# Silu by Tanh, scaled probabilities on ScalarE, an earlier residual gate and other small moves in a transformer block with a Fourier branch

## The chip, the cores and the metric

The kernel runs on one core of a Trainium2 chip. The metric is the device time of one execution in microseconds. Times of different kernels are compared by the median of several executions; one further execution is profiled.

## The reference

One layer of a block with two parallel token mixers, for 512 tokens of width 2048 and 256 context tokens, in float32:

```python
h  = modulate(rmsnorm(x, norm_g), shift, scale)         # shift, scale, gate = silu(c) @ w_ada + b_ada
hc = modulate(rmsnorm(ctx, norm_g), shift_c, scale_c)
p  = h @ w_in                  # q | k | v | z_a | u_b | z_b | g_a | g_b
attn = softmax(q k^T) v        # 12 query heads, 4 key heads, 768 keys, q and k normalized and rotated
y_a = (attn * silu(z_a)) @ w_pa
y_b = (real(fft2(u_b)) * silu(z_b)) @ w_pb
y   = (sigmoid(g_a) * y_a + sigmoid(g_b) * y_b) @ w_o
out = rmsnorm(x + gate * y, final_g)
```

## The kernel before, in words

**Precision.** Every matrix is split into a rounded part and a rest: `split_from` (L119 to L121) writes `hi` by ScalarE (L120) and `lo` by VectorE (L121), and `mm3` (L219) makes three matmuls of each product (L221 to L223). The profile names the two halves of a weight `whi` and `wlo`.

**Weights.** All weights are pieces of 128 x 1024 in one list, `todo`, in the order of their use. `start_load` issues a piece on SP's queue (L151) into a free raw tile (`wr`); `get` splits up to `len(hl_pools)` pieces ahead of the one that is asked for. A piece marked `aside` is taken out of turn by `get_aside`. Names are written in the order of the program; the framework that builds the program orders each engine's instructions, gives tiles their addresses and sets the waits. An engine then runs its instructions in that order.

**Stages.** They follow each other in the trace roughly so: modulation and the first products (to 185 us), the Fourier branch and keys and values (to 330), attention (to about 755), the products of the two sigmoid gates (to about 1065), the merge (to 1140 in its first chunks, to 1215 in all), the output product with the final norm (to the end).

**Attention.** The loop at L929 has 48 steps of 128 queries of one head (`scores`, then `turn` for the step before, then `values` for each pair). `scores` reads the maximum on VectorE (L895), makes Exp on ScalarE (L897), takes the reciprocal of the sum and scales the probabilities `p` on VectorE (L898, L899); `turn` transposes them (L906). Between these pieces `fill` advances a generator: first the 21 products of the remaining q heads and of z_a (`mtile`; `silu_into` turns z into Silu by Exp, an addition, a reciprocal and a product, L477 to L480), then the product of the Fourier branch with its weights, which writes sixteen tiles of 128 x 512 (L841, copied by ScalarE from the accumulator) and stores each by POOL's queue to `yb_d` (L842). What is left of the generator when attention ends is run by `fill(64)` (L977), with tiles of another pool, `evp`, that has four tiles of [128, 2, 512].

**The residual gate.** `gate` is a product of silu(c) with 2048 columns of w_ada. It is made on VectorE, row by row: `silu_of_row` (L672) loads half of c as a broadcast row, `crow`, and makes Silu of it by Sigmoid; `gate_piece` (L682) multiplies a 128 x 1024 weight piece by that row and sums it (L684). The first 16 pieces, for the first half of c, run in attention, one in three steps, each loaded two steps before its use. The second 16 run in the merge, where `crow` is loaded a second time; then the sums are added and stored to `gs` by POOL's queue (L1045 to L1047).

**After attention.** Eight loads on POOL's queue (L976) bring back the forms that attention stored in `f_d`. Then come four groups of seven products each (`Group`, a scheme of Strassen's kind that saves one product in eight; P1, Q5, P2, Q6, P7, Q3, Q4), whose accumulators are pairs of banks, tags "x" and "y" with two buffers each. The output product ends with a fifth such group; its last product Q4 is made token tile by token tile (`finish`, L793), and after each half `last` (L1136) forms the sums, the norm and the stores. `rms` takes a square root on ScalarE (L1117).

Of the kernel before, what the change touches and what calls it, by code (L numbers as in the profile page):

```python
# [10 lines left out]
F32 = mybir.dt.float32  # L11
# [7 lines left out]
P = 128  # L19
D = 2048  # L20
T = 512
# [61 lines left out]
def block_kernel(ctx, tc, xT, ctxT, x, c_row, w_ss, w_gate, vecs, qkg, rope, dft_c, dft_s,  # L83
# [218 lines left out]
    S = {}  # L302
    nq = KK
    for n, j in enumerate(CHUNKS):
        for pc in BRANCH_A:
            if n == 0:
                stream(("src", pc), flat(at_d[pc]), 1024, 2, dst=tiles)
            stream(("pab", j, pc), w_pab[j, pc], 1024, 2)
            if 4 <= 6 * n + pc < 20:
                stream(("gate", nq), w_gate[nq], 1024, 1, "raw")  # L310
                todo[-1].aside = True
                nq += 1
    for c in range(2):
# [160 lines left out]

    def silu_into(dst, z, tmp_pool):
        e = tmp_pool.tile([P, T], F32, tag="sil", bufs=1, name=uid("e"))
        nc.scalar.activation(e, z, ACT.Exp, scale=-1.0)  # L477
        nc.vector.tensor_scalar(e, e, 1.0, None, op0=ALU.add)
        nc.vector.reciprocal(e, e)
        nc.vector.tensor_tensor(dst, z, e, op=ALU.mult)  # L480

# [189 lines left out]

    def silu_of_row(half, row, e):  # L672

        nc.gpsimd.dma_start(row, c_row[:, 1024 * half : 1024 * half + 1024].broadcast_to([P, 1024]))
        n = e[0].shape[-1]
        for i, t in enumerate(e):
            r = row[:, n * i : n * i + n]
            nc.scalar.activation(t, r, ACT.Sigmoid)
            nc.vector.tensor_tensor(r, r, t, op=ALU.mult)
        return row  # L680

    def gate_piece(q, row, w):  # L682

        nc.vector.scalar_tensor_tensor(w, w, 1.0, row, op0=ALU.mult, op1=ALU.mult, accum_out=gparts[:, q : q + 1])  # L684

    crow = silu_of_row(0, atp.tile([P, 1024], F32, name="crow"),
                       [atp.tile([P, T], F32, tag="hs", bufs=2, name=uid("cs")) for _ in range(2)])
    later = []
# [46 lines left out]
    def job():  # L735
        if jobs:
            jobs.pop(0)()

    class Group:

# [11 lines left out]
        def run(self, name):  # L752
            form, which = next((f, c) for n, f, _, c in PRODUCTS if n == name)
            start = which not in self.acc
            if start:
                self.acc[which] = pair(self.tags[which])
            a = self.acc[which]
# [56 lines left out]
    def filler():  # L814
# [15 lines left out]
        for j in CHUNKS:  # L830
            w = [get(("pab", j, pc)) for pc in BRANCH_B]
            for t in range(4):
                acc = bank()
                a, s = t // 2, slice((t % 2) * P, (t % 2) * P + P)
                for k in range(4):
                    hi, lo = bsl[k]
                    mm3(acc, hi[:, a, s], lo[:, a, s], w[k // 2][0][:, k % 2, :], w[k // 2][1][:, k % 2, :], k == 0, k == 3)
                    if k < 3:
                        yield
                y = new_yb()  # L840
                nc.scalar.copy(y, acc)  # L841
# [44 lines left out]
    def scores(i):  # L886
# [11 lines left out]
        nc.vector.reciprocal(mx[:, 2:3], mx[:, 1:2])  # L898
        nc.vector.tensor_scalar(p, p, mx[:, 2:3], None, op0=ALU.mult)  # L899
        probs[i] = p  # L900
# [13 lines left out]
    def values(half):  # L914
        h = half // 2
        g = h // GQ
        pth, ptl = pts.pop(half)
        av = bank()
        for k in range(KT):
            s = slice(k * P, (k + 1) * P)  # L920
            mm3(av[:, :256], kvh[:, g, 1, s], kvl[:, g, 1, s], pth[:, k, :], ptl[:, k, :], k == 0, k == KT - 1)
        if half % 2 == 0:
            ats[h] = atp.tile([P, T], F32, tag="at", bufs=2, name=uid("at"))
        c = slice(256 * (half % 2), 256 * (half % 2) + 256)
        nc.vector.tensor_tensor(ats[h][:, c], av[:, :256], zs[h][:, c], op=ALU.mult)
        if half % 2 == 1:
            nc.gpsimd.dma_start(at_d[h // 2, :, h % 2, :], ats[h])

    for i in range(NSTEP + 2):  # L929
# [96 lines left out]

    crow = silu_of_row(1, slot(fm, (1024,)), [slot(fm, (1024,))])
    nq = KK
    for n, j in enumerate(CHUNKS):
# [7 lines left out]
        for pc in BRANCH_A:  # L1037
            if n == 0:
                S[pc] = get(("src", pc))
            wh, wl = get(("pab", j, pc))  # L1040
            if 5 <= 6 * n + pc < 21:
                gate_piece(nq, crow, get_aside(("gate", nq)))
                nq += 1
                if nq == 2 * KK:
                    nc.vector.tensor_tensor(gcol, gparts[:, :KK], gparts[:, KK:], op=ALU.add)  # L1045
                    nc.vector.tensor_tensor(gcol, gcol, bada[:, 2 * KK :], op=ALU.add)
                    nc.gpsimd.dma_start(gs.rearrange("k p -> p k"), gcol)  # L1047
            sh, sl = S[pc]
# [25 lines left out]
    ssq = const.tile([P, 4, 5], F32, name="ssq")  # L1074
    nc.vector.memset(ssq, 0.0)
    new_o = lambda: slot(fm, (2, 512))
# [59 lines left out]
    def last(Y, a, t):  # L1136
# [19 lines left out]
        store(tok, 0)  # L1156


    jobs.insert(0, lambda: form("A22", 0))
# [118 lines left out]
```

## Time and profile before

| | us |
|---|---|
| median of 3 runs (1420.21 to 1423.43) | 1420.81 |
| profiled execution, device time | 1417.62 |
| its span in the profile | 1415.9 |
| TensorE busy | 1367.1 |
| VectorE busy | 963.3 |
| ScalarE busy | 574.0 |
| POOL busy | 101.4 |

The profiled execution is one more run; the 1.7 us between its device time and its span lie outside what the profile covers. Engines are PE (TensorE's matmuls), PEld (its weight loads), DVE (VectorE), ACT (ScalarE), POOL and SP; L120 is line 120 of the kernel. In a group's row stand the line, the engine, the operation, output and inputs, shapes and count, then busy us and mean ns, then the idle time of the engine just before them and what ended it. In a timeline row stand start and duration in us, engine, line, operation, count, and in brackets the idle time before it with its releaser. A DMA row has the queue, the count, the KB of each and the median us from issue to landing.

### The profile page before, as it was taken

What the parts mean: (1) busy time and instruction counts of PE and PEld (TensorE: products, weight loads), DVE (VectorE), ACT (ScalarE), POOL (GpSimd) and SP (SyncE); (2) the same over time, 40 slices, a digit from 0 to 9 for tenths busy, and PEclk for the clock granted to TensorE, in tenths of its full rate; (3) what the DMA queues carried; (4) which work ended last, traced back from release to release, by engine and by line L of the source; (5) the groups of instructions that cost most, each with busy time, mean ns of one, the idle gap of its engine ahead of it and who ended that gap; (6) DMA issues with size and microseconds to landing.
All of it is one profiled execution on the core that took longest, in us unless ns stands there. A gap on an engine that the chain in (4) does not pass through costs nothing.

```text
span 1415.9 us, 17625 instructions
## 1 busy us (share of the span) xinstructions
PE 1367.1 (97%) x6842; PEld 1114.6 (79%) x6842; DVE 963.3 (68%) x1253; ACT 574.0 (41%) x785; POOL 101.4 (7%) x151
## 2 busy tenths in 40 slices
PE   6999999999999999999997999999998999999996
PEld 3667789887888888888886788888886788888874
DVE  4766596867998777777853775666857664437667
ACT  5322253534443444343443644453535122333544
POOL 0000000010011000000012101000010010000100
PEclk9999999999999999999999999999999999999998
DMA  9887453545343322232338798878899984344873
GB/s 362 322 325 273 175 182 112 175 133 169 119 142 126 105 97 83 83 97 88 121 124 351 213 296 237 265 216 255 279 277 329 334 250 139 104 134 149 180 224 131
DMA packets 73795, 275.28 MB, mean 194 GB/s; under 512 B 8560, under 2 KB 9200, under 8 KB 69232
## 3 DMA queue, kind: packets, MB, share of 16 engines
q1 hardware_dynamic: 56160, 212.54, 43.4%
q0 software_dynamic: 13808, 49.30, 13.9%
q10 hardware_dynamic: 3744, 12.32, 2.4%
q8 instruction: 53, 0.87, 0.3%
q14 instruction: 30, 0.25, 0.1%
HBM read 248.95 MB, written 25.17 MB: 194 GB/s over the span
## 4 chain that ended last, share of the span: by engine, by line
PE 70%; DMA 10%; issue 9%; DVE 8%; ACT 1%; POOL 1%; DVEq 0%; SPq 0%; POOLq 0%; ACTq 0%
PE pb L221 9%; PE pb L222 9%; PE pb L223 9%; PE x L222 6%; PE x L223 6%; PE x L221 6%; PE y L222 5%; PE y L221 5%; PE y L223 5%; DMA wr<-in_w_gate 3%; PE pd L221 2%; PE pd L223 2%; PE pd L222 2%; PE pd L392 2%; DVE wlo L121 2%
## 5 line engine op out<-in xcount | busy, mean ns | idle before, releaser
L120 ACT ACTIVATE whi<-wr 128x1024 fp32r<-128x1024 f32 x188 | 195.7, 1045 | 362.8 <-PE pb L222 91.3
L121 DVE TENSOR_TENSOR wlo<-wr,whi 128x1024 fp32r<-128x1024 f32 x188 | 225.6, 1204 | 145.0 <-ACT whi L120 144.3
L221 PE MATMUL pb<-hh,whi 128*128 128x512 f32 x512 | 207.4, 407 | 2.3 <-ACT hh L382 2.3
L222 PE MATMUL pb<-hl,whi 128*128 128x512 f32 x512 | 201.8, 394 | 0.0
L223 PE MATMUL pb<-hh,wlo 128*128 128x512 f32 x512 | 201.2, 393 | 0.0
L222 PE MATMUL y<-wlo,s 128*128 128x512 f32 x348 | 137.2, 394 | 4.4 <-DVE wlo L121 4.4
L221 PE MATMUL y<-whi,s 128*128 128x512 f32 x348 | 136.6, 392 | 2.0 <-DVE s L1144 2.0
L223 PE MATMUL y<-whi,s 128*128 128x512 f32 x348 | 136.4, 392 | 0.0
L221 PEld LDWEIGHTS pb<-hh,whi 128*128 128x128 f32 x512 | 96.6, 189 | 23.2 <-ACT hh L382 3.4
L223 PEld LDWEIGHTS pb<-hh,wlo 128*128 128x128 f32 x512 | 96.4, 188 | 22.4 <-issue 1.8
L222 PEld LDWEIGHTS pb<-hl,whi 128*128 128x128 f32 x512 | 96.9, 189 | 18.1 <-issue 1.6
L222 PE MATMUL x<-wlo,s 128*128 128x512 f32 x248 | 97.5, 393 | 2.3 <-DVE wlo L121 2.3
L221 PE MATMUL x<-whi,s 128*128 128x512 f32 x248 | 97.8, 394 | 0.0
L223 PE MATMUL x<-whi,s 128*128 128x512 f32 x248 | 97.4, 393 | 0.0
L121 DVE TENSOR_TENSOR wlo<-R,whi 128x1024 fp32r<-128x1024 f32 x59 | 71.5, 1220 | 27.6 <-ACT whi L120 27.6
L120 ACT ACTIVATE whi<-R 128x1024 fp32r<-128x1024 f32 x59 | 61.9, 1057 | 58.6 <-PE x L223 38.9
L222 PEld LDWEIGHTS y<-wlo,s 128*128 128x128 f32 x348 | 65.7, 189 | 20.9 <-DVE wlo L121 7.4
L221 PEld LDWEIGHTS y<-whi,s 128*128 128x128 f32 x348 | 65.8, 189 | 16.3 <-DVE s L1144 2.4
L223 PEld LDWEIGHTS y<-whi,s 128*128 128x128 f32 x348 | 65.7, 189 | 13.6
L897 ACT ACTIVATE p<-pd,mx 128x768 f32<-128x768 f32 x48 | 43.1, 897 | 79.4 <-DVE mx L895 79.4
L120 ACT ACTIVATE pth<-pd 128x768 fp32r<-128x768 f32 x48 | 38.9, 811 | 66.0 <-PE pd L906 66.0
L221 PE MATMUL pb<-whi,hh 128*128 128x512 f32 x144 | 57.6, 400 | 3.3 <-ACT ev L841 3.2
(287 smaller groups left out, 2735.3 us busy)
## 6 DMA issues: line engine op xcount, KB each, us to landing
wr<-in_w_g SPq DMA_DIRECT2D x80, 512.0 KB, 7.2
wa<-in_w_ss SPq DMA_DIRECT2D x32, 1024.0 KB, 7.9
wr<-in_w_m SPq DMA_DIRECT2D x44, 512.0 KB, 3.6
wr<-in_w_gate SPq DMA_DIRECT2D x32, 512.0 KB, 3.9
wr<-in_w_pab SPq DMA_DIRECT2D x32, 512.0 KB, 5.5
R<-in_w_g POOLq DMA_DIRECT2D x32, 512.0 KB, 9.8
wr<-in_w_o SPq DMA_DIRECT2D x32, 512.0 KB, 3.7
wr<-in_w_start SPq DMA_DIRECT2D x26, 512.0 KB, 6.6
```

What stands on the lines that cost most here:

```text
L120: nc.scalar.activation(hi, src, ACT.Copy)
L121: nc.vector.tensor_tensor(lo, src, hi.bitcast(F32), op=ALU.subtract)
L221: nc.tensor.matmul(o, ah, bh, start=start, stop=False, skip_group_check=cont)
L222: nc.tensor.matmul(o, ah, bl, start=False, stop=False, skip_group_check=cont)
L223: nc.tensor.matmul(o, al, bh, start=False, stop=stop, skip_group_check=cont)
L392: nc.tensor.matmul(acc[32 * j : 32 * j + 32, :256], c2[:, kk, :], w[:, k, :], start=kk < 4, stop=kk >= KK - 4)
L897: nc.scalar.activation(p, sc[:, :NKEY], ACT.Exp, bias=mx[:, 0:1], accum_out=mx[:, 1:2])
```

## The change

Seven edits are made together:

1. `silu_into` takes Tanh on ScalarE and one fused operation on VectorE, (tanh(z/2) + 1) z, which is twice Silu. The factor 1/2 goes into the product with the attention's values (L925). `silu_of_row` does the same for c, with the 1/2 in `gate_piece`.
2. The probabilities are multiplied by the reciprocal on ScalarE instead of VectorE (L899).
3. All 32 pieces of the residual gate's weight run in attention, two in three steps, each put at the front of the list one step before its use. The second row of c is loaded in step 23 into the one tile `crow`, by ScalarE's queue (the first row too); the sums are formed and stored to `gs` when the loop ends, ahead of the eight loads of the forms on POOL's queue. The merge loses its 16 pieces, its row and its store.
4. The Fourier product's tiles are pairs, [128, 2, 512]: one tile in attention instead of two half ones, whole `evp` tiles afterwards, and eight stores by ScalarE's queue instead of sixteen by POOL's.
5. In the last group the accumulators of P7 and Q4 are two pairs of which each token tile uses one bank (`Banks`); P7's subtraction is made in two pieces.
6. In the fourth gate group the two additional pairs of split tiles are given up at Q4 instead of Q3.
7. A square root of a constant is taken once after the merge, before the memset of the sums of squares, so that the table of that function is loaded there.

```diff
     for n, j in enumerate(CHUNKS):
         for pc in BRANCH_A:
...
             stream(("pab", j, pc), w_pab[j, pc], 1024, 2)
-            if 4 <= 6 * n + pc < 20:
-                stream(("gate", nq), w_gate[nq], 1024, 1, "raw")
-                todo[-1].aside = True
-                nq += 1
...
     def silu_into(dst, z, tmp_pool):
         e = tmp_pool.tile([P, T], F32, tag="sil", bufs=1, name=uid("e"))
-        nc.scalar.activation(e, z, ACT.Exp, scale=-1.0)
-        nc.vector.tensor_scalar(e, e, 1.0, None, op0=ALU.add)
-        nc.vector.reciprocal(e, e)
-        nc.vector.tensor_tensor(dst, z, e, op=ALU.mult)
+        nc.scalar.activation(e, z, ACT.Tanh, scale=0.5)
+        nc.vector.scalar_tensor_tensor(dst, e, 1.0, z, op0=ALU.add, op1=ALU.mult)
...
+    def silu_of_row(half):
+        row = atp.tile([P, 1024], F32, tag="crow", bufs=1, name=uid("crow"))
+        nc.scalar.dma_start(row, c_row[:, 1024 * half : 1024 * half + 1024].broadcast_to([P, 1024]))
+        for i in range(2):
+            r = row[:, T * i : T * i + T]
+            e = atp.tile([P, T], F32, tag="hs", bufs=2, name=uid("cs"))
+            nc.scalar.activation(e, r, ACT.Tanh, scale=0.5)
+            nc.vector.scalar_tensor_tensor(r, e, 1.0, r, op0=ALU.add, op1=ALU.mult)
         return row
...
+    class Banks:
+        def __init__(self):
+            self.b = [pair("y") for _ in range(2)]
+        def __getitem__(self, i):
+            return self.b[i[1]][i[0], 0, i[2]]
...
-                self.acc[which] = pair(self.tags[which])
+                self.acc[which] = Banks() if self.last and which == "c" else pair(self.tags[which])
...
+            elif name == "P7" and self.last:
+                for t in range(2):
+                    sub(self.V[:, t, :], self.V[:, t, :], a[:, t, :])
+                self.done(1, 1, self.V, self.V)
...
             for t in range(4):
+                if t % 2 == 0:
+                    y = new_yb()
...
-                y = new_yb()
-                nc.scalar.copy(y, acc)
-                nc.gpsimd.dma_start(yb_d[a, j, :, t % 2, :], y)
+                nc.scalar.copy(y[:, t % 2, :], acc)
+                if t % 2 == 1:
+                    nc.scalar.dma_start(yb_d[a, j], y)
                 yield
-    new_yb = lambda: atp.tile([P, T], F32, tag="hs", bufs=2, name=uid("yb"))
+    new_yb = lambda: atp.tile([P, 2, T], F32, tag="y2", bufs=1, name=uid("yb"))
...
-        nc.vector.tensor_scalar(p, p, mx[:, 2:3], None, op0=ALU.mult)
+        nc.scalar.mul(p, p, mx[:, 2:3])
...
-        if i < 3 * KK - 2 and i % 3 == 0:
-            todo.insert(0, Piece(("gate", i // 3), [w_gate[i // 3]], 1024, 1, "raw"))
+        if i % 3 > 0 and i < 3 * KK:
+            q = i // 3 * 2 + i % 3 - 1
+            gate_piece(q, crow, get_aside(("gate", q)))
+        if i == 3 * KK // 2 - 1:
+            crow = silu_of_row(1)
+        if i % 3 < 2 and i < 3 * KK:
+            q = i // 3 * 2 + i % 3
+            todo.insert(0, Piece(("gate", q), [w_gate[q]], 1024, 1, "raw"))
             todo[0].aside = True
-        elif i < 3 * KK and i % 3 == 2:
-            gate_piece(i // 3, crow, get_aside(("gate", i // 3)))
         fill(4 - i % 2)
+    nc.vector.tensor_tensor(gcol, gparts[:, :KK], gparts[:, KK:], op=ALU.add)
+    nc.vector.tensor_tensor(gcol, gcol, bada[:, 2 * KK :], op=ALU.add)
+    nc.gpsimd.dma_start(gs.rearrange("k p -> p k"), gcol)
...
-    new_yb = lambda: new_ev()[:, 0, :]
+    new_yb = new_ev
...
             elif (g, name) == (3, "Q3"):
                 raw_pools.pop()
+            elif (g, name) == (3, "Q4"):
                 hl_pools[:] = [p for p in hl_pools if not isinstance(p, int)]
...
+    nc.scalar.activation(ssq[:, 0, 0:1], eps_t, ACT.Sqrt)
+    nc.vector.memset(ssq, 0.0)
```

More of the change, by code (lines that the diff above doesn't have):

```diff
@@ L302, in block_kernel @@
     S = {}
-    nq = KK
     for n, j in enumerate(CHUNKS):
@@ L670, in block_kernel @@
                                        gq[:, None, a, :].broadcast_to([P, 4, HD]), op0=ALU.mult, op1=ALU.mult)
[L672 to L679, printed above, removed]
+    def silu_of_row(half):
[6 more added lines that the diff above has]
+            nc.vector.scalar_tensor_tensor(r, e, 1.0, r, op0=ALU.add, op1=ALU.mult)
         return row
     def gate_piece(q, row, w):
-        nc.vector.scalar_tensor_tensor(w, w, 1.0, row, op0=ALU.mult, op1=ALU.mult, accum_out=gparts[:, q : q + 1])
-    crow = silu_of_row(0, atp.tile([P, 1024], F32, name="crow"),
-                       [atp.tile([P, T], F32, tag="hs", bufs=2, name=uid("cs")) for _ in range(2)])
+        nc.vector.scalar_tensor_tensor(w, w, 0.5, row, op0=ALU.mult, op1=ALU.mult, accum_out=gparts[:, q : q + 1])
+    crow = silu_of_row(0)
     later = []
@@ L924, in values @@
         c = slice(256 * (half % 2), 256 * (half % 2) + 256)
-        nc.vector.tensor_tensor(ats[h][:, c], av[:, :256], zs[h][:, c], op=ALU.mult)
+        nc.vector.scalar_tensor_tensor(ats[h][:, c], av[:, :256], 0.5, zs[h][:, c], op0=ALU.mult, op1=ALU.mult)
         if half % 2 == 1:
@@ L1025, in form @@
         mf[name][4 * h : 4 * h + 4] = split_form(comb[name, h] if src is None else src, pool)
-    crow = silu_of_row(1, slot(fm, (1024,)), [slot(fm, (1024,))])
-    nq = KK
     for n, j in enumerate(CHUNKS):
@@ L1040, in block_kernel @@
             wh, wl = get(("pab", j, pc))
[L1041 to L1047, printed above, removed]
             sh, sl = S[pc]
@@ L1074, in block_kernel @@
     ssq = const.tile([P, 4, 5], F32, name="ssq")
-    nc.vector.memset(ssq, 0.0)
     new_o = lambda: slot(fm, (2, 512))
```

## The prediction

> **What bounds the kernel now.** I read the page first, then the waits of TensorE (PE), then its work in stretches, then the rows around each pause.
>
> ```profile
> span 1415.9 us, 17625 instructions
> ...
> PE 1367.1 (97%) x6842; PEld 1114.6 (79%) x6842; DVE 963.3 (68%) x1253; ACT 574.0 (41%) x785; POOL 101.4 (7%) x151
> ```
>
> TensorE is busy 97% of the span and the change leaves its matmuls alone, so it can only give or take pauses. Who TensorE waited for (total, times, longest):
>
> ```profile
> PE x L221 <- ACT whi L120: 8.6, 2, 6.8
> ...
> PE pb L221 <- ACT ev L841: 3.2, 1, 3.2
> ...
> PE y L221 <- DVE s L1144: 2.0, 1, 2.0
> PE pd L221 <- DVE ptl L121: 1.6, 1, 1.6
> ```
>
> The waits are few and each has a place. Stretches (us; busy of PE, PEld, DVE, ACT, POOL with instructions; granted clock; DMA share; GB/s), from two queries:
>
> ```profile
> 345.00:745.00 400.00, 398.03 (x2196) 342.03 (x2195) 315.95 (x447) 161.51 (x248) 30.95 (x50) 1.00 0.34 109
> 760.27:789.23 28.96, 18.16 (x61) 13.55 (x61) 15.56 (x16) 14.05 (x19) 2.94 (x6) 0.82 0.83 319
> 790.00:1018.00 228.00, 228.00 (x1007) 188.48 (x1006) 156.39 (x164) 114.28 (x138) 21.50 (x25) 1.00 0.87 254
> ```
> ```profile
> 1075.00:1092.00 17.00, 13.24 (x48) 9.58 (x47) 14.77 (x14) 9.93 (x10) 0.00 (x0) 0.90 0.98 359
> 1116.00:1131.00 15.00, 11.86 (x44) 8.99 (x43) 11.62 (x17) 2.11 (x2) 0.00 (x0) 0.89 0.92 355
> ```
>
> Undisturbed, 1007 matmuls take 228 us: 0.226 us each. By that price the 60 matmuls between the last attention work and the first pieces of the gate products need 13.6 us and took 28.96: **15.4 us lost**. Around 1075 to 1092, 48 matmuls need 10.9 and took 17: **6.1 lost**. Around 1116 to 1131, 44 need 10.0 and took 15: **5.0 lost**. Attention (345 to 745) loses only 2 of its 400 us, though VectorE is busy there for 316. So VectorE's relief in attention is worth almost nothing in itself; what counts is what happens at the other three places and at the very end.
>
> **Part 1, the end of attention.** The rows that lose the 15.4 us:
>
> ```profile
> 759.59 1.06 ACT L120 ACTIVATE s<-s 128x1024 fp32r<-128x1024 f32 x1 [4.87 <-DMA s<-f_d]
> ...
> 769.07 1.04 ACT L120 ACTIVATE whi<-R 128x1024 fp32r<-128x1024 f32 x1
> 778.15 0.58 ACT L841 COPY ev<-pb 128x512 f32<-128x512 f32 x1 [8.04 <-DMA yb_d<-ev]
> ...
> 780.04 1.06 ACT L120 ACTIVATE whi<-R 128x1024 fp32r<-128x1024 f32 x1
> ```
> ```profile
> 763.59 0.50 PE L221 MATMUL pb<-whi,hh 128*128 128x512 f32 x1 [3.16 <-ACT ev L841]
> ...
> 781.16 0.80 PE L221 MATMUL x<-whi,hh 128*128 128x512 f32 x1 [6.76 <-ACT whi L120]
> ...
> 783.86 0.63 PE L222 MATMUL x<-wlo,hh 128*128 128x512 f32 x1
> ```
> ```profile
> s<-f_d POOLq DMA_DIRECT2D x7, 512.0 KB, 14.7
> ...
> yb_d<-yb POOLq DMA_DIRECT2D x11, 256.0 KB, 2.3
> yb_d<-ev POOLq DMA_DIRECT2D x5, 256.0 KB, 13.6
> ...
> crow<-in_c_row POOLq DMA_DIRECT2D x1, 512.0 KB, 5.8
> ...
> gs<-gcol POOLq DMA_DIRECT2D x1, 8.0 KB, 13.2
> ```
>
> ScalarE works in order. Five copies of the Fourier product (L841) need a tile of the four in `evp`; one holds a form, so the fourth copy waits 8.04 us for an earlier copy's store. That store is queued on POOL behind the eight form loads and lands after 13.6 us, where the eleven stores before those loads took 2.3. Behind the copy stands the split of the third weight piece (780.04), and TensorE waits 6.76 us for it. After such a pause matmuls run at 0.63 us instead of 0.39 for a while. With whole [P, 2, T] tiles the last copies need two `evp` tiles at most, so no copy waits for a store; the eight stores of 512 KB leave POOL's queue for ScalarE's.
>
> What is late next: the split of the second piece stands at 769.07, behind form splits that wait for loads (759.59). Nothing moves those loads forward, and I assume that ScalarE's order stays. From 760.27 the last twelve Fourier matmuls and twelve of the first piece, 24 x 0.226, bring TensorE to 765.7, where it waits for 769.07 + 1.04 = 770.1: 4.4 us. Beside the pauses of 3.16 and 6.76 us, 5.5 of the 15.4 went into the slow matmuls behind them and small waits, half of it, 2.7, for each; with one pause left, 4.4 + 2.7 = 7.1 stay: **gain 8.3**. Bounds: 15.4 if the order improves, 3 if the forms come later. They can: the store of `gs` now goes out on POOL ahead of the eight form loads; it adds between nothing and its whole 13.2 us to landing. I take little, since it is 8 KB.
>
> **Part 2, merge.** Sixteen gate pieces leave this stage.
>
> ```profile
> L684 DVE SCALAR_TENSOR_TENSOR wr<-wr,s 128x1024 f32<-128x1024 f32 x16 | 19.6, 1225 | 16.9 <-DMA wr<-in_w_gate 16.7
> ```
> ```profile
> 1126.42 0.50 PE L222 MATMUL x<-wlo,s 128*128 128x512 f32 x1 [2.32 <-DVE wlo L121]
> ...
> 1140.11 0.88 PE L1006 MATMUL y<-ident,g 128*128 128x128 f32 x6 [0.91 <-DVE g L1058]
> ```
>
> VectorE spent 19.6 us on them and stood 16.7 us still for their weights; the `wlo` that TensorE waited for at 1126.42 and the sums at 1140.11 were queued behind. That group goes whole: 5.0 + 0.9 = 5.9. The pauses at 1075 to 1092 hang on late `at_d` loads while the DMA share is 0.98; 8 MB of weights, a broadcast row and a Sigmoid leave, and two more split tiles stay through Q3, but the `at_d` loads stay where they are. I take half of 6.1, 3.0 (bounds 0 and 6.1). **Gain 8.9.**
>
> **Part 3, attention.** Durations for what changes:
>
> ```profile
> L897 ACT ACTIVATE p<-pd,mx 128x768 f32<-128x768 f32 x48 | 43.1, 897 | 79.4 <-DVE mx L895 79.4
> ...
> L479 DVE RECIPROCAL e<-e 128x512 f32<-128x512 f32 x12 | 40.2, 3349 | 0.2
> ...
> L899 DVE TENSOR_SCALAR p<-p,mx 128x768 f32<-128x768 f32 x48 | 29.7, 619 | 1.1
> ...
> L480 DVE TENSOR_TENSOR z<-pb,e 128x512 f32<-128x512 f32 x12 | 8.1, 678 | 0.0
> ```
>
> VectorE: the reciprocals go (40.2, and a small add each); one fused operation costs about the 678 ns of the product it replaces; the scalings go (29.7); 16 gate pieces come (19.6). 316 - 40 - 30 + 20 = 266 of 400. ScalarE: 48 scalings, which the trace does not show in this form; nearest is the Exp of the same size, 0.897, so 161.5 + 43 = 205 of 400. The path from scores to transposes lengthens by 0.897 - 0.619 = 0.28 us a step, plus waiting. Its cover, shown by one early and one later step (scaled, then transposed):
>
> ```profile
> 357.05 0.61 DVE L899 TENSOR_SCALAR p<-p,mx 128x768 f32<-128x768 f32 x1
> ...
> 359.93 0.38 PE L906 MATMUL pd<-ident,p 128*128 128x128 f32 x2
> ```
> ```profile
> 506.51 0.62 DVE L899 TENSOR_SCALAR p<-p,mx 128x768 f32<-128x768 f32 x1
> ...
> 515.28 0.38 PE L906 MATMUL pd<-ident,p 128*128 128x128 f32 x2
> ```
>
> These stand 2.27 and 8.15 us apart, so 0.28 is covered and I charge nothing for it.
>
> The ScalarE page of the Trainium skill (ScalarE: Activation LUTs, Rules for kernel authors) says the opposite of this edit: a multiplication belongs on VectorE, not on ScalarE. The rows agree that one operation is dearer there, 897 against 619 ns; charged to the path by that rule, 48 x 0.28 = 13.3 us would come off the sum, and 7.0 would stay of 20.3.
>
> Three new waits on ScalarE: the second `c_row` load is issued from its queue behind gate piece 15 and lands after 5.8 us, with Exp and weight splits queued behind; a copy into the single Fourier tile waits for the store before it, at least 2.3 us; each scaling waits for VectorE's reciprocal. The first outlasts the smaller cover: 0 to 5 us, once; the second some 0 to 2. Gate loads come one step ahead of use instead of two, and 32 of them pass SP's queue among the weights; DMA share 0.34 hides them. Against that the 1.6 us of the waits' last row goes with VectorE's relief. **Gain 1.0**, between 2.0 (all that the stretch loses) and -6.
>
> **Part 4, the end.**
>
> ```profile
> 1398.71 1.28 ACT L1117 ACT_TABLE_LOAD   x1
> ...
> 1399.60 0.51 PE L221 MATMUL y<-whi,s 128*128 128x512 f32 x1 [1.99 <-DVE s L1144]
> ...
> 1405.28 0.75 DVE L1155 SCALAR_TENSOR_TENSOR s<-s,r,s 128x512 f32<-128x512 f32 x1
> 1406.97 0.76 DVE L1144 TENSOR_TENSOR s<-y,s 128x256 f32<-128x256 f32 x2 [0.94 <-PE y L223]
> ```
>
> The second half's matmuls wait 1.99 us for VectorE to have read the first half out of the same accumulator. With two accumulators they go on at 1399.60 - 1.99 = 1397.6, and 24 of them at 0.226 end near 1403.0, 3.9 us before VectorE got them (1406.97). Then VectorE is late: its work on the first half ends at 1405.28 + 0.75 = 1406.03, and the table load, now made long before, takes 1.28 out of that: 1404.75 instead of 1406.97. The early load falls where ScalarE has room (9.93 of 17 us at 1075 to 1092); if Copy or Square behind it changed the table again, the 1.28 would be back. That is 2.2; P7's subtraction in two pieces costs about 0.1. **Gain 2.1** (bounds 0.9 and 3.9).
>
> **The sum.** 8.3 + 8.9 + 1.0 + 2.1 = 20.3 us. The profiled execution took 1417.62 us (1.7 beside its span) and would take 1397.3; the median of the runs, 1420.81, lies 0.2% above it, and the same gain there gives 1400.5.
>
> **The rivals.** *The stall moves* (0.2): form loads land later behind `gs`, or ScalarE stays blocked by them, so part 1 gives 3 and the first merge group nothing: 3 + 5.9 + 2.1 = 11, 1410. For it: the 4.87 us at 759.59. Against: the first forms were being split at 759.59, before even the first product began. *Everything comes back* (0.14): 15.4 + 6.1 + 5.9 + 3.9 + 2.0 = 33.3, 1387. For it: all pauses have a named cause that the change touches. Against: DMA shares of 0.83 and 0.98, so the data itself is late. *ScalarE becomes attention's brake* (0.07): it waits in order for a reciprocal queued behind a gate piece of 1.225 us, and weight splits and probabilities behind it are late; from 0.40 us of TensorE lost per step (the other parts' 19.3 / 48) the change is no gain. At 1.225 in each of 32 steps with a gate piece it costs 39.2: 1420.8 - 19.3 + 39.2 = 1441. For it: more waiting on one in-order engine; against: 8.15 us of cover, 205 busy of 400. (The Trainium skill's rule on multiplications, above, leans this way.) *It does not do what it says* (0.03): Tanh beside Exp could need a table load each way, 24 x 1.28 = 31 us on ScalarE; if two thirds of it reached TensorE, all 20.3 would be eaten: 1421.
>
> The Trainium skill (ScalarE: Activation LUTs, Table sets: the hidden batching unit) lists tanh in Exp's set, so by it there is no switch; no run yet shows a Tanh.
>
> **How the numbers follow.** The forecast as described has 0.56, its own range 1394 to 1407. With the stall that moves and most of the case of full return the range is 1388 to 1413. About 0.2% (2.8 us) can be told from no change. Faster: 0.56 + 0.2 + 0.14 less a tenth of unfavourable tails, 0.89; slower 0.07; same 0.04.
>
> **What would show it.** Right: no ScalarE copy L841 waiting for `yb_d`, no pause over 5 us between 755 and 790, no waits for `wlo` or the merged sums where 1116 to 1140 stood, VectorE near 266 and ScalarE near 205 us over attention, and the table load far from the end. Wrong: new pauses of TensorE before transposes or scores, or before Q5 with forms as the releaser.

## The result and the profile after

| | before | after |
|---|---|---|
| median of the runs compared, us | 1422.12 | 1407.92 |
| profiled execution, device time | 1417.62 | 1406.39 |
| its span | 1415.9 | 1404.3 |

The change is faster: after takes 0.990 of before (95% interval 0.9882 to 0.9918), 14.2 us. The forecast was 1400.5 within 1388 to 1413, 20.3 us. So the sign and the range held, but the sum hides two errors of opposite sign: the end of attention, which was to give 8.3 us, lost 4.1, and the merge gave 13.2 for 8.9. That they offset each other in part is luck: 1407.92 lies just outside the 1394 to 1407 that the prediction gave to its own mechanism, and near the 1410 of its rival "the stall moves". One run of a later kernel (late splits and sums) took 2414.39 us at a granted clock of 0.696, where every other run had 0.982 or more, and is left out of that kernel's median.

Where the time went is seen by taking the same matmul in both traces (there are 6842 in every kernel) and asking how much earlier it starts. Differences of that lead, in us, positive is won:

| stretch of before | forecast | after |
|---|---|---|
| attention, 345 to 750 | 1.0 | 1.1 |
| end of attention, 750 to 822 | 8.3 | -4.1 |
| first merge group, 1060 to 1095 | 3.0 | 6.7 |
| second merge group, 1095 to 1160 | 5.9 | 6.5 |
| 1160 to the end | 2.1 | 0.6 |

With 0.8 ahead of attention this is the 11.6 us between the spans. After's line numbers are shifted: L850 is the Fourier copy (L841 before), L852 its store, L909 the scaling, L474 the fused half of Silu, L679 the gate piece (L684), L1125 the square root (L1117), L1152 and L1163 stand for L1144 and L1155. L120, L121 and L185 stay: hi by ScalarE, lo by VectorE, sum of two raw tiles by VectorE.

The page of after, and who TensorE waited for (three of the lines):

```profile
span 1404.3 us, 17554 instructions
...
PE 1358.6 (97%) x6842; PEld 1110.5 (79%) x6842; DVE 896.2 (64%) x1185; ACT 614.2 (44%) x837; POOL 91.6 (7%) x133
```
```profile
PE x L221 <- ACT whi L120: 9.5, 2, 7.8
...
PE x L222 <- DVE wlo L121: 7.4, 3, 6.0
...
PE y L222 <- DVE wlo L121: 1.5, 3, 0.7
```

The waits for `ev`, for the merged `g` and for `s` are gone. What is left behind the first 345 us is almost all in two pauses. The stretches, with the columns as in the prediction:

```profile
345.00:745.00 400.00, 399.04 (x2198) 342.39 (x2197) 266.82 (x410) 201.93 (x297) 27.29 (x42) 1.00 0.43 132
760.00:795.00 35.00, 18.73 (x69) 14.08 (x68) 24.52 (x23) 19.10 (x24) 1.76 (x2) 0.76 0.87 311
1060.00:1137.00 77.00, 77.00 (x349) 63.91 (x349) 43.58 (x42) 29.90 (x35) 4.80 (x10) 1.00 0.74 269
```

VectorE came to 267 us over attention and ScalarE to 202, as forecast (266, 205). The two merge groups run with no pause at all. In the 35 us after attention TensorE is busy for half, at a granted clock of 0.76. Here is ScalarE in that stretch, then VectorE, then TensorE:

```profile
766.74 0.63 ACT L120 ACTIVATE hh<-wr 128x512 fp32r<-128x512 f32 x1 [5.77 <-DMA wr<-in_w_g]
767.27 1.04 ACT L120 ACTIVATE whi<-R 128x1024 fp32r<-128x1024 f32 x1
...
770.45 1.15 ACT L120 ACTIVATE hh<-wr 128x512 fp32r<-128x512 f32 x2 [1.61 <-DMA wr<-in_w_g]
771.50 1.99 ACT L120 ACTIVATE s<-s 128x1024 fp32r<-128x1024 f32 x2
773.40 1.54 ACT L850 COPY ev<-pb 128x512 f32<-128x512 f32 x3
...
779.12 1.99 ACT L120 ACTIVATE whi<-R 128x1024 fp32r<-128x1024 f32 x2
```
```profile
778.15 1.23 DVE L185 TENSOR_TENSOR wr<-wr,wr 128x1024 f32<-128x1024 f32 x1 [0.27 <-DMA wr<-in_w_g]
779.29 3.49 DVE L121 TENSOR_TENSOR s<-s,s 128x1024 fp32r<-128x1024 f32 x3
784.60 1.23 DVE L185 TENSOR_TENSOR wr<-wr,wr 128x1024 f32<-128x1024 f32 x1 [1.82 <-DMA wr<-in_w_g]
785.74 1.22 DVE L121 TENSOR_TENSOR wlo<-R,whi 128x1024 fp32r<-128x1024 f32 x1
```
```profile
780.22 0.79 PE L221 MATMUL x<-whi,hh 128*128 128x512 f32 x1 [7.81 <-ACT whi L120]
...
787.01 0.80 PE L222 MATMUL x<-wlo,hh 128*128 128x512 f32 x1 [6.00 <-DVE wlo L121]
```

No copy L850 into a tile of `evp` waits for a store any more, as forecast. (Ahead of that, in attention, four copies into the single pair tile wait for its store, 10.1 us in all; TensorE lost nothing visible by it.) But other work now stands ahead of P1's fourth piece, the `whi` at 779.12. On ScalarE these are `hh<-wr`, splits of P2's pieces, which wait 5.77 and 1.61 us for weights that have not landed; the forms and copies pile up behind them. On VectorE it is `wr<-wr,wr`, sums for P7, a product four places later. The second of them comes behind three rests of forms, waits for a load until 784.60, and P1's `wlo` stands right behind it. P1's own weights had landed long before: the four loads were issued by 749.24, and the last landed at 758.60.

The weights of P2 are not later than they were. In before the same split stands at 767.58, released by the same load:

```profile
767.58 0.63 ACT L120 ACTIVATE hh<-wr 128x512 fp32r<-128x512 f32 x1 [1.94 <-DMA wr<-in_w_g]
```

Three of the loads behind it are issued 3.5 to 5 us later in after, since their raw tiles wait for the last store of the pair tile (landed at 759.81). All six weight pieces that follow P1's (issued from 751.36 to 760.79) still land within 0.8 us of before. What moved is the work around them: in before one half of P2 stands ahead of P1's third piece and the rest behind it, and P7's first sum comes at 790.34, behind all of P1.

By the lead of the matmuls, the copies' vanished waits gave 12 us by the second of the old pauses, and the two new ones, with the slow matmuls behind them, took 16.5.

### The profile page after: what moved, and what is told of

It reads as the page before. It is cut to its first block, busy times and chain, and to the rows that moved or that the text cites. A ratio compares the mean times of both kernels' runs of the same rounds, so it can differ in the third digit from the quotient of the medians.

```text
span 1404.3 us, 17554 instructions
## 1 busy us (share of the span) xinstructions
PE 1358.6 (97%) x6842; PEld 1110.5 (79%) x6842; DVE 896.2 (64%) x1185; ACT 614.2 (44%) x837; POOL 91.6 (7%) x133
## 4 chain that ended last, share of the span: by engine, by line
PE 89%; DMA 4%; DVE 3%; ACT 1%; issue 1%; SPq 0%; DVEq 0%; ACTq 0%
PE pb L221 12%; PE pb L222 12%; PE pb L223 12%; PE x L222 7%; PE x L223 7%; PE x L221 7%; PE y L223 6%; PE y L222 6%; PE y L221 6%; PE pd L221 3%; PE pd L223 3%; PE pd L222 3%; PE pd L916 2%; PE pd L387 2%; DMA wr<-in_w_g 2%
## 5 line engine op out<-in xcount | busy, mean ns | idle before, releaser
L121 DVE TENSOR_TENSOR wlo<-wr,whi 128x1024 fp32r<-128x1024 f32 x188 | 226.1, 1206 | 183.3 <-ACT whi L120 182.3
L120 ACT ACTIVATE whi<-wr 128x1024 fp32r<-128x1024 f32 x188 | 195.8, 1045 | 332.9 <-PE y L223 89.7
L120 ACT ACTIVATE whi<-R 128x1024 fp32r<-128x1024 f32 x57 | 59.8, 1057 | 62.9 <-PE x L223 37.8
L121 DVE TENSOR_TENSOR wlo<-R,whi 128x1024 fp32r<-128x1024 f32 x57 | 69.2, 1221 | 25.8 <-ACT whi L120 25.8
L121 DVE TENSOR_TENSOR ptl<-pd,pth 128x768 fp32r<-128x768 f32 x48 | 45.8, 954 | 30.1 <-ACT pth L120 30.1
```

The costliest lines, as they stand in the source:

```text
L120: nc.scalar.activation(hi, src, ACT.Copy)
L121: nc.vector.tensor_tensor(lo, src, hi.bitcast(F32), op=ALU.subtract)
```

## The experiments

Two theories of the end of attention. **A, order:** what stands ahead of P1's pieces on the in-order ScalarE and VectorE sets the time; the framework placed work there whose data is late. **B, data:** the DMA engines are full after attention, and the time is set by what they have brought, whatever the order.

**The change in four parts.** Each kernel is before with the edits named, nothing else (only with edit 3, `silu_of_row` takes Tanh as in the change).

> The kernel before with edits 1 and 2 alone (Silu by Tanh for z_a, probabilities scaled on ScalarE; the row of c keeps its Sigmoid). Both theories of the end of attention (A: later products' splits and sums stand ahead of the first product's on ScalarE and VectorE; B: the loads there are late because the DMA engines are full) say nothing happens behind attention. In attention: gain 1 to 2 us, as forecast, since TensorE lost only 2 of 400; VectorE 316 - 70 = 246, ScalarE 161.5 + 45 = 206. If the whole change owes more to these two than the 1.9 us by which its attention came out shorter, the time falls by over 4 us. Expected: 1418 to 1421, most likely 1419.5.

> The kernel before with edit 3 alone (all 32 gate pieces in attention, Silu of c by Tanh, sums stored to gs ahead of the form loads). If the 13.4 us gained in the merge belong to this edit, the time falls by 12 to 14 us, less what it costs at the end of attention. Theory A: if this edit turned the order there, the end of attention loses up to 5 us: 1413 to 1416; if not, 1407 to 1410. Theory B and the store of gs ahead of the loads as brake: the forms land later than before, counted from the last value product, and the first split of a form starts later than 9 us behind it. Half of the first merge group only, as I forecast: 1412.

> The kernel before with edit 4 alone (Fourier product in whole tiles, stored by ScalarE's queue). My forecast's step: no copy waits for a store any more and one pause stays: 8.3 us less, 1412.5. Theory A: the copies no longer wait, but splits and sums of later products whose loads have not landed come ahead of the first product's third and fourth pieces; nothing is gained or up to 5 us are lost at the end of attention: 1420 to 1426. Theory B: the stores go out earlier and add to the transfers between 755 and 785; the pauses end on loads of the first product's own data.

> The kernel before with edits 5, 6 and 7 alone. The end: the wait of 1.99 us for VectorE goes, but the end hangs on VectorE behind its work on the first half, so 0.9 to 2.1 us; the table load of the square root is seen at the kernel's beginning and again near the end, so its 1.28 us are not gained. Edit 6 (split tiles kept through Q3 of the last gate group): if the first merge group's gain comes from it, up to 6 us at 1060 to 1099; if it came from the gate pieces that left, none. Expected: 1419 without that, 1413 with it.

Measured against before, and the same stretches as above from the profiles:

| | edits 1, 2 | edit 3 | edit 4 | edits 5 to 7 | all |
|---|---|---|---|---|---|
| ratio | 0.9998 | 0.9919 | 1.0031 | 1.0014 | 0.990 |
| interval | 0.9982 to 1.0014 | 0.9903 to 0.9935 | 1.0016 to 1.0045 | 1.0000 to 1.0028 | 0.9882 to 0.9918 |
| attention | -0.2 | 1.5 | -0.2 | -1.8 | 1.1 |
| end of attention | 0.7 | -0.3 | -4.8 | 0.1 | -4.1 |
| first merge group | -0.6 | -0.4 | -1.4 | 5.5 | 6.7 |
| second merge group | -4.9 | 6.5 | -4.9 | -11.6 | 6.5 |
| to the end | -1.0 | -1.4 | -1.3 | 1.0 | 0.6 |

The gain of 1 to 2 us expected of edits 1 and 2 did not come, and edits 5 to 7 missed their 1413 to 1419 us with 1424.57. Three things follow. First, the loss at the end of attention is edit 4's alone; its trace shows the same two pauses and one before them (of 1.70 us in after):

```profile
770.51 0.79 PE L221 MATMUL x<-whi,hh 128*128 128x512 f32 x1 [3.60 <-ACT whi L120]
...
781.23 0.80 PE L221 MATMUL x<-whi,hh 128*128 128x512 f32 x1 [4.79 <-ACT whi L120]
...
787.35 0.80 PE L222 MATMUL x<-wlo,hh 128*128 128x512 f32 x1 [5.33 <-DVE wlo L121]
```

Second, the parts' ratios add up to only 5 us of gain; 9 more come when the edits stand together. By the traces these belong to edits 3 and 6, though no kernel has these two alone. With edits 5 to 7, edit 6 wins the first merge group, and it is lost again behind, where a gate piece that edit 3 would have moved waits on VectorE (edits 5 to 7; VectorE, then TensorE):

```profile
1115.55 1.22 DVE L684 SCALAR_TENSOR_TENSOR wr<-wr,s 128x1024 f32<-128x1024 f32 x1 [5.28 <-DMA wr<-in_w_gate]
...
1116.70 1.22 DVE L121 TENSOR_TENSOR wlo<-wr,whi 128x1024 fp32r<-128x1024 f32 x1
```
```profile
1117.97 0.50 PE L222 MATMUL y<-wlo,s 128*128 128x512 f32 x1 [3.29 <-DVE wlo L121]
```

Third, the three profiles that keep the sixteen pieces in the merge (edits 1 and 2, edit 4, edits 5 to 7) show there one pause more than the profile of before. A split waits for a load of `w_pab`, which in before came just in time; the pause and the slow matmuls behind it cost each of them 5.6 us or more (edits 1 and 2; ScalarE, then TensorE):

```profile
1157.90 1.06 ACT L120 ACTIVATE whi<-wr 128x1024 fp32r<-128x1024 f32 x1 [17.84 <-DMA wr<-in_w_pab]
```
```profile
1159.01 0.50 PE L221 MATMUL x<-whi,s 128*128 128x512 f32 x1 [2.81 <-ACT whi L120]
```

None of the kernels with edit 3 shows it. So the profile of before understates what the merge can lose, which fits its 1417.62 us beside medians of 1421 to 1422.

**Edit 6 inside the whole.**

> The changed kernel without edit 6 (the additional split tiles given up at Q3 again). Alone, edit 6 shortened the time to the first merge group by 4.9 us and lost as much behind it; edit 3 alone left the pauses at 1073 to 1082 (5.6 us) as they were. If the first merge group's gain belongs to edit 6, the pauses of 1.3 to 2.1 us before x<-whi,hh and x<-wlo,hh come back near 1065 to 1080 and the time is 5 to 7 us longer than the changed kernel's: 1414. If it belongs to the 8 MB of gate weights that left, as half of it did in my forecast, the time stays within 1.5 us or loses 3.

```diff
             elif (g, name) == (3, "Q3"):
                 raw_pools.pop()
-            elif (g, name) == (3, "Q4"):
                 hl_pools[:] = [p for p in hl_pools if not isinstance(p, int)]
```

1416.54 us, 0.9958 (0.9942 to 0.9974): 8.6 us longer than the changed kernel's 1407.92. The stretch 1060 to 1095, first without edit 6, then the changed kernel:

```profile
1060.00:1095.00 35.00, 29.43 (x117) 22.97 (x116) 24.27 (x24) 16.30 (x18) 0.00 (x0) 0.90 0.82 294
```
```profile
1060.00:1095.00 35.00, 35.00 (x156) 28.96 (x156) 26.98 (x28) 18.14 (x21) 0.00 (x0) 1.00 0.84 304
```

39 matmuls more in the same 35 us at nearly the same DMA share. The first group's gain is edit 6's, not the lighter DMA load's. How it comes about is seen on ScalarE, first without edit 6, then in the changed kernel:

```profile
1082.81 1.06 ACT L120 ACTIVATE s<-wr 128x1024 fp32r<-128x1024 f32 x1 [4.56 <-DMA wr<-at_d]
1083.78 1.04 ACT L120 ACTIVATE whi<-R 128x1024 fp32r<-128x1024 f32 x1
```
```profile
1072.98 1.14 ACT L120 ACTIVATE hh<-R 128x512 fp32r<-128x512 f32 x2
```

Without the two tiles Q4's third piece is split behind a piece of `at_d` whose load is late. With them its second and third pieces are split by 1077.1, and the waits for `at_d` (5.86 us at 1088.71) hold up nothing that TensorE needs.

**Edit 4 undone inside the whole.**

> The changed kernel without edit 4 (Fourier product in half tiles, stored by POOL's queue, as before). Edit 4 alone was 4.4 us slower by the medians, and its loss lies at the end of attention. If that holds inside the whole change, this one takes 4 to 5 us less than the changed kernel: 0.987 of before instead of 0.990, about 1403; the pauses at the end of attention are those of before (3.2 at the copy, 6.8 at the third piece) instead of 7.8 and 6.0. If the loss there is due to load by the other edits (rival B, full DMA engines), it stays within 1 us of the changed kernel.

1402.63 us, 0.9884 (0.9866 to 0.9903), 5.3 us less than the whole change by the medians. The intervals of the two ratios overlap; by the profiles the end of attention loses 0.4 us here instead of 4.1. So edit 4 costs about what it costs alone, as expected.

**The order changed, the loads kept or moved.** Four kernels on the changed one; all edits concern the first group.

> The changed kernel with the two additional pairs of split tiles given to the weights from P2 on instead of Q5 on, in the first group. Then no split of P2's pieces (hh) can stand ahead of P1's on ScalarE, but P7's two sums (L185) still stand ahead of P1's last rest on VectorE. Loads and their volume stay. Theory A: ScalarE's part of the stall goes, VectorE's stays: the 7.8 us wait for whi shrinks, the wait for wlo behind the sums whose loads land near 784 stays, so 0 to 3 us less than the changed kernel: 1405 to 1408. Theory B: no change at all, since the transfers are the same: 1408.

```diff
-            if (g, name) == (0, "Q5"):
+            if (g, name) == (0, "P2"):
                 hl_pools += range(MORE_HL)
```

1418.57 us, 0.9986 (0.997 to 1.0001), 10.7 us longer than the changed kernel. Both expectations miss: B says no change, and I had A gain a little. The trace shows why (VectorE, then TensorE):

```profile
780.16 1.23 DVE L185 TENSOR_TENSOR wr<-wr,wr 128x1024 f32<-128x1024 f32 x1 [13.56 <-DMA wr<-in_w_g]
```
```profile
791.08 0.80 PE L222 MATMUL x<-wlo,hh 128*128 128x512 f32 x1 [18.22 <-DVE wlo L121]
```

With P2's splits out of the way, VectorE comes to P7's sum earlier and stands 13.56 us before it, with P1's rest queued behind: TensorE waits 18.22 us at one stroke. That is A's mechanism at its plainest. It makes up half of what this kernel loses against the changed one; the other half goes at 819.55, where TensorE waits 3.64 us for a piece of P2 behind another two-part sum (817.14, 5.96 us for its load).

> As the kernel with late splits, and the two raw tiles of evp are given to the loads from P2 on too, in the first group. Now neither P2's splits nor P7's sums can stand ahead of P1's pieces. Theory A: both pauses of 7.8 and 6.0 us and the slow matmuls behind them go, up to what Q5's own data allows: 8 to 13 us less than the changed kernel, 1395 to 1400. Theory B: the four tiles of P7 (2 MB, 5 us at the 410 GB/s seen there) are moved, no more: 5 us at most, and the wait comes back later at P7.

```diff
-    raw_pools.append((evp, 2, "raw", 2))
...
-            if (g, name) == (0, "Q5"):
+            if (g, name) == (0, "P2"):
+                raw_pools.append((evp, 2, "raw", 2))
+            if (g, name) == (0, "P2"):
                 hl_pools += range(MORE_HL)
```

1410.23 us, 0.9933 (0.9914 to 0.9952): the 1395 to 1400 of A did not come. The matmuls that the changed kernel starts at 795 us start 12.3 us earlier, all that A promised, but by 822 us it is given back, and the merge groups win 3.6 us less than there. What gives it back is again order and late data together: two-part sums, whose loads were held back, stand in VectorE's way, first ahead of a piece of Q5 (785.42), then, for longest, ahead of a piece of P2 (VectorE, then TensorE):

```profile
805.81 1.22 DVE L185 TENSOR_TENSOR wr<-wr,wr 128x1024 f32<-128x1024 f32 x1 [5.99 <-DMA wr<-in_w_g]
806.95 1.22 DVE L121 TENSOR_TENSOR wlo<-wr,whi 128x1024 fp32r<-128x1024 f32 x1
```
```profile
808.22 0.79 PE L222 MATMUL x<-wlo,hh 128*128 128x512 f32 x1 [4.98 <-DVE wlo L121]
```

> The changed kernel with only the two raw tiles of evp given to the loads from Q5 on: the order on ScalarE and VectorE stays as in the changed kernel through P1 (splits of P2 and sums of P7 ahead), but their loads come later by up to two tiles. Theory A: the engines stand behind loads that come later, so no gain, and up to 5 us slower: 1408 to 1413. Theory B: fewer transfers beside P1's, so 2.5 us or more faster: 1405 or less.

The raw tiles of `evp` go to the loads from Q5 on, no other edit. 1407.6 us, 0.9909 (0.9894 to 0.9924): as the changed kernel, with the pauses at 779.30 (5.45) and 786.60 (6.50). B's 2.5 us do not come; A's extra loss does not either, since the loads hardly moved.

> The changed kernel with the additional split tiles from P2 on (as the kernel with late splits), and the two-part sums of P7 (L185) of the first group made by POOL instead of VectorE. All loads stay where the changed kernel has them; only what stood ahead of P1's splits and rests on ScalarE and VectorE is gone. Theory A (order): the end of attention comes out some 12 us shorter, as in the kernel with late splits and late loads, and since the loads are not held back, more than the 0.1 us that was left there at 822 us stays: 8 us, 1400 (1396 to 1403). Theory B (the data of the next products sets the time by 822 us, whatever the order): all of it is given back in Q5 to P7, 1406 to 1410.

```diff
-            nc.vector.tensor_tensor(src, src, r, op=ALU.add)
+            (nc.gpsimd if e.key[:2] == ("P7", 0) else nc.vector).tensor_tensor(src, src, r, op=ALU.add)
...
-            if (g, name) == (0, "Q5"):
+            if (g, name) == (0, "P2"):
                 hl_pools += range(MORE_HL)
```

1415.52 us, 0.9951 (0.9935 to 0.9966). Again 10 us are won by 795 us, and 13 lost by 822, more than B expected. POOL is the third in-order queue: Q6's weights are added in memory by DMAs that POOL issues (`R<-in_w_g`), and these now stand behind its sums (POOL, ScalarE, TensorE):

```profile
780.83 2.82 POOL L185 TENSOR_TENSOR wr<-wr,wr 128x1024 f32<-128x1024 f32 x1 [23.46 <-DMA wr<-in_w_g]
787.69 2.87 POOL L185 TENSOR_TENSOR wr<-wr,wr 128x1024 f32<-128x1024 f32 x1 [4.04 <-DVE s L121]
790.51 3.56 POOL L194 DMA_DIRECT2D R<-in_w_g  x4
```
```profile
801.12 1.15 ACT L120 ACTIVATE hh<-R 128x512 fp32r<-128x512 f32 x2 [15.27 <-DMA R<-in_w_g]
```
```profile
803.27 0.79 PE L221 MATMUL x<-whi,hh 128*128 128x512 f32 x1 [8.78 <-ACT whi L120]
```

**The square root's table.** Edit 4 is undone here too.

> The kernel without edit 4, with the early square root made to read a merged tile (scale 0), so that it can't be placed at the kernel's beginning. The table load then stands at the end of the merge and none is left near the end. My step 7: 1.28 us of the end are gained: 1401.3 instead of 1402.6. If Copy or Square behind it changed the table again, the load is seen near the end as before and nothing is gained.

```diff
...
-    nc.scalar.activation(ssq[:, 0, 0:1], eps_t, ACT.Sqrt)
+    nc.scalar.activation(ssq[:, 0, 0:1], merged[CHUNKS[-1], 1][:, 0, 0:1], ACT.Sqrt, bias=eps_t[:, 0:1], scale=0.0)
```

1403.46 us, 0.9871 (0.9852 to 0.989), against 1402.63 without it: the two can't be told apart, and the 1.28 us expected are not seen. In the trace the load stands at the end of the merge, the square root follows the squares with no load between, and from the first of these squares to VectorE's last instruction it takes 12.6 us (1384.08 to 1396.69) instead of 13.0 (1382.55 to 1395.54): 0.4 of the 1.28.

```profile
1385.32 0.62 ACT L1123 ACTIVATE r<-r,eps_t 128x1 f32<-128x1 f32 x2
```

That VectorE's other work covers the rest is not shown. A pause of 2.11 us before scores in attention, with slow matmuls behind it, took the 0.4 back in this execution.

**An order without the late pieces.** Without edit 4, the half tiles share whole `evp` tiles after attention, and all stores go out by ScalarE's queue; the late square root is kept.

> The kernel without edit 4 and with the late square root, in which the Fourier product's half tiles share whole evp tiles once attention is over, and all its stores go out by ScalarE's queue. In the instruction order this gives, no copy waits for a store, P1's second and third pieces are split ahead of any piece of P2, its fourth behind three halves of P2 (whose loads landed at 766 to 771 in the changed kernel), and P7's sums come behind all of P1 on VectorE. Theory A (order): the pauses of 3.2 and 7.3 us at the end of attention go, but for 1 to 3 us, and some of that stays: 1395 to 1400 by the median. Theory B for what follows (by 822 us the accumulated weights of Q6 set the time, whatever the order before): what is won by 795 us is given back by 822 us, and the time is that of the two kernels it is made of, 1402 to 1403.

The main lines of the diff, against the kernel without edit 4:

```diff
-                y = new_yb()
+                if late[0]:
+                    if t % 2 == 0 or not held:
+                        held[:] = [new_ev()]
+                    y = held[0][:, t % 2, :]
+                else:
+                    y = atp.tile([P, T], F32, tag="hs", bufs=2, name=uid("yb"))
                 nc.scalar.copy(y, acc)
-                nc.gpsimd.dma_start(yb_d[a, j, :, t % 2, :], y)
+                nc.scalar.dma_start(yb_d[a, j, :, t % 2, :], y)
```

1393.16 us, 0.9797 (0.9779 to 0.9815): 28 us less than before, 14.8 less than the changed kernel, and under the lower end that I had given for A. ScalarE, POOL's first accumulating DMA, and the stretch:

```profile
759.72 1.06 ACT L854 COPY ev<-pb 128x512 f32<-128x512 f32 x2
...
762.43 1.06 ACT L120 ACTIVATE whi<-R 128x1024 fp32r<-128x1024 f32 x1 [0.17 <-PE pb L223]
...
765.47 1.06 ACT L120 ACTIVATE whi<-R 128x1024 fp32r<-128x1024 f32 x1
766.43 1.66 ACT L120 ACTIVATE hh<-wr 128x512 fp32r<-128x512 f32 x3
767.99 1.05 ACT L120 ACTIVATE whi<-R 128x1024 fp32r<-128x1024 f32 x1
```
```profile
774.44 0.90 POOL L194 DMA_DIRECT2D R<-in_w_g  x1 [20.02 <-DVE wlo L121]
```
```profile
757.00:792.00 35.00, 28.29 (x117) 22.90 (x117) 25.08 (x24) 21.41 (x27) 3.47 (x4) 0.95 1.04 359
```

P1's pieces are split without a pause of TensorE before them, the same `hh<-wr` come between without a wait, and Q6's additions leave at 774.44 instead of 789.53 in the changed kernel. The DMA engines move 359 GB/s here at a share of 1.04, against 311 at 0.87 in the changed kernel: they had room there, and B falls as the main cause. By 822 us the kernel stands 6.7 us better than before over the end of attention, where the changed kernel is 4.1 worse. Two pauses are left, both behind data that is late: 3.32 us at 760.35, for copies behind form splits that wait for their loads, as before, and 3.39 us at 790.36, behind a P7 sum that waits 5.26 us for its load. This kernel differs from the one with the late square root (1403.46) only in how the Fourier tiles are placed and stored, and takes 10.3 us less.

What stays open: why the framework's order turned with edit 4 was not tried apart from the kernels above. That the queue of the stores is not the reason is shown by the last kernel, which has ScalarE's queue too and a good order.

## Why the prediction was right and wrong

**Part 1, wrong in sign.** The mechanism named was real: the copies' waits for stores at the end of attention went with edit 4. But one of the signs that the prediction set for itself, no pause over 5 us between 755 and 790, is missing: there are pauses of 7.81 and 6.00 us. The step that failed is the sentence "I assume that ScalarE's order stays". The change alters tiles and queues, the framework orders anew, and what it put ahead of P1's pieces had its data later than they. The prediction listed what is late next only among the instructions in their old order. The rival "the stall moves" was nearer in its time, though not in its cause: it left a gain of 3 here and put the blame on loads behind `gs`; but the form loads were issued at 749.03 (750.80 before), and edit 3 alone lost 0.3 there. The Trainium skill (TensorE: Matmul & The Clock Gate, Architectural detail: the array is 16× 32×32, not 1× 128×128) says that ScalarE and VectorE take their instructions strictly in order; the traces agree, with 13.56 us of VectorE standing before one sum (late splits) while finished data lay behind it.

**Part 2, right in kind, too small, and half of it for the wrong reason.** The second group gave 6.5 for the 5.9 forecast, by edit 3, as named. Of the first group I took half of 6.1, by a guess on the DMA load; it came whole (6.7), and the two split tiles kept through Q3, named there in half a sentence, make all of it. The late `at_d` loads were read rightly, and they stay late; what I missed is that with two more tiles Q4's pieces need not wait behind them. Edit 6 needed a term of its own.

**Part 3, right that nothing is lost; the number is chance.** Attention gave 1.1 us for the 1.0 forecast, but the reason named, VectorE's relief, gave -0.2 by itself (edits 1 and 2). Edit 3, which was charged as a cost, shows 1.5, and edits 5 to 7, which change nothing in this stretch, show -1.8: a difference of 1 us there can't be told from none. The price of the scaling, in after:

```profile
L909 ACT ACTIVATE p<-p,mx 128x768 f32<-128x768 f32 x48 | 45.0, 937 | 11.2 <-DVE mx L908 11.0
```

The scaling takes 937 ns for the 897 taken from Exp, and waits 11 us in all for the reciprocal, at no cost to the whole: edits 1 and 2 alone leave the time where it was (0.9982 to 1.0014). By the Trainium skill's rule that a multiplication belongs on VectorE (ScalarE: Activation LUTs, Rules for kernel authors) up to 13.3 us would have been lost; the measurement decides, and the cover that the two early and late rows showed held. Nor is there a table load between Exp and Tanh, as the Trainium skill has it (ScalarE: Activation LUTs, Table sets: the hidden batching unit): no load stands at L473.

**Part 4, near for another reason than the one given.** The two accumulators work: the pause of 1.99 us between Q4's halves is gone (two of 0.48 and 0.35 us for `wlo` are left), the matmuls end early, and VectorE is late, as forecast (the second half's L1152 runs right behind the first half's L1163). VectorE's last instruction ends 12.9 us earlier than before, 1.9 of them won behind 1160, for 2.1 forecast; the last store then took 5.8 us to the end of the span for 4.5 before, which leaves 0.6. That store took 4.5 us in the three kernels with neither edit 3 nor edits 5 to 7, before among them, and 4.8 to 5.8 in all others; why stays open. The failed term is the table load. The early square root reads only a constant; the framework put it at the kernel's start, other tables followed, and the load stands where it stood:

```profile
1386.83 1.28 ACT L1125 ACT_TABLE_LOAD   x1
```

In its place the waits for `wlo` near the end shrank, to 2.1 us in all from 3.2; that this makes up the difference is not shown. Moved for good, the load is worth 0.4 only. (It then stands at 1220.89, behind the merge, and not at 1075 to 1092, where the prediction looked for ScalarE's room.) The rival that the change doesn't do what it says was given for Tanh; it came true for this small edit instead. ScalarE as attention's brake did not come.

## What to carry to other kernels

A stall that is taken off an in-order engine is worth only what the next instruction on it allows. Where a framework chooses the order, a change of tiles or queues reorders it: compare the instruction order of both programs around the stall, and ask of each instruction ahead of the critical one when its own data lands. Price every edit that keeps or frees a buffer by itself and together with the edit that clears the engine behind it: here edit 6 was worth nothing with edits 5 and 7 alone, and 8.6 us in the whole change, where edit 3 had cleared what stands behind it.

## What the runs showed of the hardware that was not expected

Pauses of TensorE of 2 to 3.4 us may or may not be followed by a stretch at half clock (the granted clock is 0.50 from 775 to 780 in the changed kernel, within its pause of 7.81 us). Two rows of stretches, the first behind a pause of 2.11 us (late square root), the second around one of 2.08 us (edit 3 alone); the granted clock is the third number from the end:

```profile
726.00:735.00 9.00, 7.28 (x34) 6.25 (x35) 2.79 (x5) 5.89 (x10) 1.62 (x3) 0.81 0.41 133
```
```profile
1080.00:1086.00 6.00, 4.22 (x18) 3.49 (x19) 5.60 (x6) 4.13 (x4) 0.00 (x0) 1.00 0.97 306
```

The matmuls behind the first run at 0.81 of the clock: 0.19 of 9 us, doubled, is 3.4 us at half speed. In the changed kernel's 35 us at 0.76 it is 16.8, five times that. In the kernel without the late pieces even the pause of 3.39 us at 790.36 left the granted clock at 1.00 (786 to 800). And with the sums on POOL, one instruction of VectorE beside each sum took 3.23 and 3.41 us instead of 1.22 (POOL's sums run from 780.83 and 787.69 there; the second is one of the two at 787.10):

```profile
781.51 3.23 DVE L121 TENSOR_TENSOR wlo<-R,whi 128x1024 fp32r<-128x1024 f32 x1
...
787.10 4.55 DVE L121 TENSOR_TENSOR wlo<-R,whi 128x1024 fp32r<-128x1024 f32 x2
```
